# An encoder layer on one core: score products of the linear attention gathered in two visits a chunk, mLSTM scores placed behind the state products, output weights and gate transposes moved forward

## The chip, the cores and the metric

The kernel runs on one core of a Trainium2 chip. The metric is the device time of one execution in microseconds. The core's engines are TensorE (PE, matrix products), VectorE (DVE), ScalarE (ACT), GpSimd (POOL) and SyncE (SP, which here issues nearly all transfers). Each runs its own list of instructions in order and waits on semaphores for the others. Matrix products write to PSUM, which has eight banks of 512 numbers for each of the 128 partitions. TensorE's clock is granted by a throttle; the profile shows it as a share of full speed.

## The reference

One layer on 1024 tokens of width 1024. Token mixing: RMS norm, one input projection whose columns feed two groups of four heads, both scanned forward and backward with the directions summed, a norm for each head, a gate, one output projection, RMS norm, residual. Channel mixing: RMS norm, a gated MLP of width 2816 with a depthwise convolution of three taps, RMS norm, residual.

```
def hybrid_mixer(hn, w_in, ...):
    proj = jnp.matmul(hn, w_in).astype(jnp.float32)
    a_qk, a_v, a_o, a_gates, b_q, b_k, b_v, b_r, b_lr = jnp.split(proj, idx, axis=-1)
    ...
    y_a = jax.nn.sigmoid(a_o) * head_rms_norm(h_fw + h_bw, mlstm_norm).reshape(bsz, s, A_V)
    ...
    y_b = jax.nn.silu(b_r) * head_rms_norm(o_fw + o_bw, gla_norm).reshape(bsz, s, B_V)
    return jnp.matmul(jnp.concatenate([y_a, y_b], axis=-1), w_out)
```

The mLSTM group (a) has one decay for each token and head, so its scores are one product times a matrix of decays. The gated linear attention (GLA, group b) has a decay for each key dimension:

```
    diff = b[..., :, None, :] - b[..., None, :, :]
    decay = jnp.exp(jnp.where(causal, diff, -jnp.inf))
    s = jnp.einsum('bhtd,bhsd,bhtsd->bhts', q_, k_, decay)
```

## The kernel before, in words

The kernel works in chunks of 128 tokens (c = 0 to 7), with forward and backward on the two halves of the partitions. Products of full precision are made of three: high times high, high times low, low times high part.

Two Python generators, `proj()` and `mix()`, give the work until the output projection. `_interleave` takes a step of whichever has the smaller sum of weights, so the weights (`R_AUX`, `R_COLS`, `R_GLA`, `R_STATES`, `R_ML`, `R_OUT`, each times `W_PROJ`) set how many steps of projections go between two steps of the mixers. The order in which the generators issue is a first order; a scheduler behind them fixes the final list of each engine.

`proj()` holds the input projections that are left after the first stage. They fill TensorE while the mixers' other engines work: 384 products of 512 columns (`facc`, `f_block`) for keys and queries, then 1344 of 256 columns (`tacc`, `t_block`) for values and gates. Here they are called fillers.

`mix()` goes through these stages:

- `gla_decay()` and `gate_rows()`: the decays of both groups. `gate_rows` adds biases, takes logarithms, scans and exponentials on rows of 36 partitions (`gi`, `gf`, `rm`), and then transposes them in TensorE, chunk by chunk (`ptc`), into columns `cols`.
- `gla()`: `levels(0)`; `states()` (key transposes `ptk`, state products `U`, running states `slots`); then for each chunk `levels(c+1)` and `finish(c)`. `levels` builds the 128 x 128 scores from eight levels L = 64, 32, 16, 8, 4, 2, 1, 0. `weigh(L)` forms differences `D` on GpSimd, exponentials `E` on ScalarE, and weighted queries `Q` and keys (`K` for 32, the zero-padded `kz[L]` for 16 to 1) on VectorE. `pair_up` multiplies them into a PSUM tile `sc`. `keep` copies the tile into `Pt` or `acc` on ScalarE (64, 32, 16) or with a predicated copy on VectorE (8 and below). `finish` makes the output `o` from `Pt`, the decayed queries and the state, and its head norm.
- `mlstm()`: `states()` (keys by DMA, transposes `ptm`, state products `Um`, running states `mslots`), then for each chunk `decays(c)` (loads of keys `kko`, broadcast decay rows `RB` and `RI`, queries `qq`; 1.4 MB by DMA), `front(c)` (scores `sr`, weighed into `RB`) and `back(c)` (products `nd` with values and states, then `hs`, its norm and its store to `dya`).
- `out_weights()`: eight rows of output weights, 0.5 MB each, are loaded into `oraw`, multiplied by the gains and split into `woh` (ScalarE) and `wol` (VectorE); then `prep(0)` loads the mixers' results and gates (`yv`, `gv`), multiplies them and transposes them (`pt`) for the output projection (`oacc`).

Behind the interleaved part stand the output projection and channel mixing, which the change leaves alone.

## Time and profile before

| what | value |
| --- | --- |
| three runs | 1189.73, 1193.89 (median), 1195.28 us |
| the profiled execution | 1189.67 us, its span 1187.9 us |
| mean granted TensorE clock | 0.989 |
| busy: PE, DVE, ACT, POOL | 1151.1, 878.7, 591.4, 166.5 us |
| projections and gates | about 48 to 146 us |
| GLA: level products of chunk 0 and states, then the chunks | 129 to 183, 183 to 297 us |
| mLSTM: states, then the chunks | 304 to 323, 327 to 409 us |
| rest of the projections and output weights | 409 to 440 us |
| output projection | 440 to 575 us |
| channel mixing | 575 to 1188 us |

A row of groups reads: line, engine, operation, output and inputs by the program's names, shapes, count, then busy time, mean nanoseconds of one, and the idle time before them with what ended it. A row of the timeline or of the chain begins with its start and its length. L182 is line 182 of the kernel before. Matmuls are pipelined: each is shown with its full length, and the step from one start to the next is what it costs TensorE. Busy time of PE therefore contains the short gaps between matmuls that do not follow at the full rate.

### The profile page before, as it was taken

How to read it: one execution, taken by the hardware profiler on the slowest of the kernel's cores; microseconds unless marked ns; L12 is line 12 of the kernel's file. 1: busy time of each engine (PE TensorE's matmuls, PEld its weight loads, DVE VectorE, ACT ScalarE, POOL GpSimd, SP SyncE). 2: the span in 40 equal slices, each digit the busy share in tenths (PEclk: the TensorE clock that was granted, in tenths of full speed). 3: DMA queues.
4: the chain of work that ended last, by engine and by line, in shares of the span. 5: the costliest groups of instructions: out<-in, count | busy, mean ns of one | idle time of the engine just before them, and what ended most of it. 6: DMA issues, size and time to landing. Idle time of an engine off the chain costs nothing.

```text
span 1187.9 us, 21230 instructions
## 1 busy us (share of the span) xinstructions
PE 1151.1 (97%) x7896; PEld 979.7 (82%) x7896; DVE 878.7 (74%) x1604; ACT 591.4 (50%) x1271; POOL 166.5 (14%) x240
## 2 busy tenths in 40 slices
PE   8999999999999969999999999999999999999997
PEld 7989778888989968878788888888888878888885
DVE  5676669777433557667998888888888877987666
ACT  6572686878556534446543243433433245445451
POOL 1200425665054200101000000000000000000001
PEclk9999999999989989999999999999999999999999
DMA  7453675554777385542144342333224238754245
GB/s 201 149 134 102 169 223 155 152 171 127 189 197 209 117 278 186 178 141 80 36 142 142 109 132 64 113 123 108 89 81 133 98 123 299 252 178 133 81 137 190
DMA packets 134651, 175.77 MB, mean 148 GB/s; under 512 B 24964, under 2 KB 89860, under 8 KB 134548
## 3 DMA queue, kind: packets, MB, share of 16 engines
q1 hardware_dynamic: 134116, 172.58, 47.3%
q0 software_dynamic: 432, 1.84, 0.4%
q8 instruction: 62, 1.02, 0.3%
q14 instruction: 41, 0.34, 0.1%
HBM read 126.78 MB, written 47.53 MB: 147 GB/s over the span
## 4 chain that ended last, share of the span: by engine, by line
PE 73%; DVE 7%; ACT 6%; DMA 6%; issue 3%; POOL 3%; SPq 1%; DVEq 0%; POOLq 0%; ACTq 0%
PE pr L1063 35%; PE pr L1221 17%; PE facc L171 5%; PE oacc L1002 4%; PE tacc L182 4%; PE vacc L262 2%; DMA qq<-dmqq 1%; DMA yv<-dya 1%; DMA oraw<-in_w_out_dram 1%; DVE kz L637 1%; ACT sq L543 1%; DVE slots L537 1%; POOL RB L786 1%; POOL D L621 1%; POOL D L622 1%
## 5 line engine op out<-in xcount | busy, mean ns | idle before, releaser
L1063 PE MATMUL pr<-T,ah 128*128 128x512 f32 x704 | 217.2, 389 | 1.3 <-DVE G L1101 1.3
L1063 PE MATMUL pr<-B,ah 128*128 128x512 f32 x528 | 162.8, 390 | 0.0
L1063 PEld LDWEIGHTS pr<-T,ah 128*128 128x128 f32 x704 | 132.1, 188 | 29.4 <-DVE G L1101 1.8
L1063 PE MATMUL pr<-T,al 128*128 128x512 f32 x352 | 137.0, 389 | 0.0
L182 PE MATMUL tacc<-wh,xh 128*128 128x256 f32 x448 | 130.5, 291 | 0.0
L182 PE MATMUL tacc<-wl,xh 128*128 128x256 f32 x448 | 130.0, 290 | 0.0
L182 PE MATMUL tacc<-wh,xl 128*128 128x256 f32 x448 | 127.1, 284 | 0.0
L1221 PE MATMUL pr<-dwl,dah 128*128 128x512 f32 x308 | 120.0, 390 | 0.7 <-DVE dwl L113 0.7
L1221 PE MATMUL pr<-dwh,dal 128*128 128x512 f32 x308 | 120.1, 390 | 0.0
L1221 PE MATMUL pr<-dwh,dah 128*128 128x512 f32 x308 | 119.3, 390 | 0.0
L1063 PEld LDWEIGHTS pr<-B,ah 128*128 128x128 f32 x528 | 99.0, 188 | 20.4
L1063 PE MATMUL pr<-B,al 128*128 128x512 f32 x264 | 102.7, 389 | 0.0
L112 ACT CAST dah<-ar 128x512 fp32r<-128x512 f32 x77 | 47.6, 621 | 98.0 <-PE pr L1221 44.2
L182 PEld LDWEIGHTS tacc<-wh,xh 128*128 128x128 f32 x448 | 85.5, 191 | 2.7 <-issue 0.2
L182 PEld LDWEIGHTS tacc<-wl,xh 128*128 128x128 f32 x448 | 85.5, 191 | 1.4
L182 PEld LDWEIGHTS tacc<-wh,xl 128*128 128x128 f32 x448 | 85.7, 191 | 0.3
L112 ACT CAST ah<-fraw 128x512 fp32r<-128x512 f32 x64 | 39.6, 619 | 82.7 <-PE pr L1063 49.7
L113 DVE TENSOR_TENSOR dal<-ar,dah 128x512 fp32r<-128x512 f32 x77 | 53.0, 690 | 37.0 <-ACT dah L112 36.7
L1063 PEld LDWEIGHTS pr<-T,al 128*128 128x128 f32 x352 | 66.1, 188 | 13.6
L112 ACT CAST ah<-sa 128x512 fp32r<-128x512 f32 x44 | 27.4, 622 | 83.6 <-DVE sa L943 52.9
L1221 PEld LDWEIGHTS pr<-dwl,dah 128*128 128x128 f32 x308 | 57.8, 188 | 13.1 <-DVE dwl L113 1.1
L1221 PEld LDWEIGHTS pr<-dwh,dal 128*128 128x128 f32 x308 | 57.8, 188 | 12.9 <-DVE dal L113 0.9
(292 smaller groups left out, 2536.0 us busy)
## 6 DMA issues: line engine op xcount, KB each, us to landing
ar<-dA SPq DMA_DIRECT2D x77, 256.0 KB
wraw<-in_w_in_dram SPq DMA_DIRECT2D x48, 256.0 KB
fraw<-in_ffn_w_gate_dram SPq DMA_DIRECT2D x22, 512.0 KB
fraw<-in_ffn_w_up_dram SPq DMA_DIRECT2D x22, 512.0 KB
dA<-s SPq DMA_DIRECT2D x20, 512.0 KB
dA<-sx SPq DMA_DIRECT2D x10, 768.0 KB
Y<-in_ffn_w_down_dram SPq DMA_DIRECT2D x22, 256.0 KB
S<-dS SPq DMA_DIRECT2D x16, 258.0 KB
```

What stands on the lines that cost most here:

```text
L112: nc.scalar.copy(out=hi, in_=src)
L113: nc.vector.tensor_tensor(out=lo, in0=src, in1=hi.bitcast(F32), op=ALU.subtract)
L171: nc.tensor.matmul(acc, w[:, k, cs], v[:, k, hs], start=(k == 0 and n == 0), stop=(k == NK - 1 and n == 2))
L182: nc.tensor.matmul(acc[:, i, :], v[:, k, ts], w[:, k, :], start=(k == 0 and n == 0), stop=(k == NK - 1 and n == 2))
L262: nc.tensor.matmul(acc, v[:, k, ts], w[:, k, :], start=(k == 0 and n == 0), stop=(k == NK - 1 and n == 2))
L537: nc.vector.scalar_tensor_tensor(out=sl[rs, o, h, :], in0=sl[rs, c, h, :], scalar=sc(c, h)[rs], in1=sl[rs, o, h, :], op0=ALU.mult, op1=ALU ...
L543: nc.scalar.activation(sq, o[:, h, :], AF.Square, accum_out=ss[:, h:h + 1])
L621: nc.gpsimd.tensor_tensor(out=dv[:, :, :, 0, :], in0=ref, in1=xv[:, :, :, 0, :], op=ALU.subtract)
L622: nc.gpsimd.tensor_tensor(out=dv[:, :, :, 1, :], in0=xv[:, :, :, 1, :], in1=ref, op=ALU.subtract)
L1002: nc.tensor.matmul(accs[hf], v[:, j, :], w[:, k, hf * 512:(hf + 1) * 512], start=(k == 0 and n == 0), stop=(k == NK - 1 and n == 2))
L1063: nc.tensor.matmul(acc, A[i][:, k, :], B[b][j][:, k, :], start=(k == 0 and n == 0), stop=(k == 3 and n == 2))
L1221: nc.tensor.matmul(accs[i], o[v][:, ts], o[w], start=(p == 0 and n == 0), stop=(p == NP - 1 and n == 2))
```

## The change

Five things change, with the values computed staying the same.

1. **GLA scores in groups.** `products` takes up to five levels. The group's first is (64, 32, 16), which share one PSUM bank of 512 columns; the second is (8, 4, 2, 1, 0), which takes a bank and a quarter. `hold` puts the first product of a group behind a named instruction of the list, the weighing of the level after the group. For chunks 1 to 6 the second group, its copies and the last copies into `Pt` are put off (`owed`) until level 64 of the next chunk has been weighed. `Q` has eight buffers in place of three. The differences of each level are held behind the last filler issued so far (`pace`).
2. **mLSTM scores behind state products.** `front(c+1)` is issued directly behind the last `nd` product of chunk c, its weighing one step later. `decays(0)` and `decays(1)` are issued within the states, keys are loaded two chunks ahead, the next keys are transposed behind the state products, and `v` is loaded in `front`. `mslots` moves into the pool `ml`.
3. **Output weights.** Three of the eight rows get a pool of their own and are loaded at chunks 4, 5 and 6 of the mLSTM; each further row is loaded as soon as one has been split. `gpost` and the loads of `prep(0)` come earlier, the latter when the first half of the gates is done.
4. **Weights of the interleaving.** `R_AUX` 3.4 to 3.0, `R_GLA` 0.7 to 0.8, `R_ML` 1.9 to 1.7, `R_OUT` 2.0 to 1.3.
5. `yh` and `yl` of the output projection get a pool of their own.

```diff
-R_AUX, R_COLS, R_GLA, R_STATES, R_ML, R_OUT = 3.4, 0.6, 0.7, 0.7, 1.9, 2.0
+R_AUX, R_COLS, R_GLA, R_STATES, R_ML, R_OUT = 3.0, 0.6, 0.8, 0.7, 1.7, 1.3
...
+        def hold(ins, after):
+            tc.add_manual_dep(ins.ins, after.ins.name, mybir.DependencyInfo(mybir.DependencyClass.NoSync, mybir.DependencyReason.DATA),
+                              reason="one visit")
...
-                def products(pair):
-                    scs = [(L, pair_up(L, *qk)) for L, qk in pair]
+                def products(group, last):
+                    scs, room, first = [], 0, None
+                    for L, (Q, K, _) in group:
+                        n = 256 if L == 64 else 128
+                        if room < n:
+                            bank, room = ps.tile([P, 512], F32, name="sc", tag="ps"), 512
+                        sc = bank[:, 512 - room:512 - room + n].rearrange("p (h t) -> p h t", h=H)
+                        room -= n
+                        m = pair_up(L, Q, K, sc)
+                        first = first or m
+                        scs.append((L, sc))
+                    hold(first, last)
                     for L, sc in scs:
                         keep(L, sc)
...
                 due = []
-                for n, L in enumerate((64, 32, 16, 8, 4, 2, 1, 0)):
+                for L in (64, 32, 16, 8, 4, 2, 1, 0):
                     due.append((L, weigh(L)))
-                    if n % 2 == 0 and n:
-                        products(due[:2])
-                        due = due[2:]
+                    if L == 64 and c - 1 in owed:
+                        owed.pop(c - 1)(due[0][1][2])
+                    if L == 8:
+                        products(due[:3], due[3][1][2])
+                        due = due[3:]
                     yield
...
+                if 0 < c < NC - 1:
+                    owed[c] = lambda last: rest(group, last)
+                else:
+                    rest(group, end)
...
+                        with tc.issue_after(ins.ins):
+                            nxt = keys(*loaded[n + 1])
...
                     yield
+                    if n in (4, 6):
+                        decays(n // 2 - 2)
                     yield
...
             yield from states()
-            decays(0)
-            decays(1)
             yield R_ML * W_PROJ
-            front(0)
+            front(0)()
             for c in range(NC):
                 if c + 2 < NC:
                     decays(c + 2)
-                if c + 1 < NC:
-                    front(c + 1)
+                if NC - 4 <= c < NC - 1:
+                    load_raw(c - NC + 4)
+                ins = back(c)
+                after = front(c + 1, ins) if c + 1 < NC else None
                 yield
-                back(c)
+                if after:
+                    after()
                 yield
...
+    def load_raw(k):
+        if "raw" not in ow:
+            ow["raw"] = right.enter_context(tc.tile_pool(name="orw", bufs=3, side="right", reuse_waits="tile"))
+        raws[k] = ow["raw"].tile([P, D], F32, name="oraw")
+        nc.sync.dma_start(raws[k], w_out[:, k, :])
...
         for k in range(NK):
-            raw = op.tile([P, D], F32, name="oraw", tag=("yv", "yv", "gv")[k % 3], bufs=(2, 2, 1)[k % 3])
-            nc.sync.dma_start(raw, w_out[:, k, :])
-            split_scaled(woh[:, k, :], wol[:, k, :], raw, hg[:, k, :])
+            split_scaled(woh[:, k, :], wol[:, k, :], raws.pop(k), hg[:, k, :])
+            if k + 3 < NK:
+                load_raw(k + 3)
             yield
+        nc.sync.dma_start(gpost, rows_of(a["norm_mix_post"][0]))
+        while "half" not in done:
+            yield
+        first = prep(0)
+        next(first)
         while "gate" not in done:
             yield
-        for _ in prep(0):
+        for _ in first:
             pass
-        nc.sync.dma_start(gpost, rows_of(a["norm_mix_post"][0]))
```

What the lists of the engines make of it stands at three places. The first is TensorE in the GLA loop, the levels below 16 of a chunk and what surrounds them (`sc` the scores, `tacc` a filler, `o` the chunk's output). Before, eight or more fillers stand between one level and the next:

```order
L182 MATMUL tacc<-wh,xh 128x256
L656 MATMUL sc<-Q,kz_1445 32x32 x16
L182 MATMUL tacc<-wl,xh 128x256
L182 MATMUL tacc<-wh,xl 128x256
...
L656 MATMUL sc<-Q,kz_1446 32x32 x16
L654 MATMUL sc<-qq,kk 32x32 x16
L182 MATMUL tacc<-wh,xh 128x256
L699 MATMUL o<-v,Pt 128x128
L700 MATMUL o<-slots,qd 128x128
```

After the change the five levels stand together:

```order
L184 MATMUL tacc<-wh,xh 128x256
L661 MATMUL sc<-Q,kz_1400 32x32 x16
L661 MATMUL sc<-Q,kz_1401 32x32 x16
L661 MATMUL sc<-Q,kz_1402 32x32 x16
L661 MATMUL sc<-Q,kz_1403 32x32 x16
L659 MATMUL sc<-qq,kk 32x32 x16
L184 MATMUL tacc<-wl,xh 128x256
```

Of the runs of attention products that fillers separate there were 110 up to the output projection, and there are 67.

The second place is ScalarE's list from the last rows of `gate_rows` to the first columns (`cols` is the copy of `ptc`, `stg<-tacc` the copy of a finished filler block of 48 products). Before:

```order
L361 ACTIVATE rm<-rm 36x1024
L359 ACTIVATE gf<-gf 36x1024
L357 ACTIVATE lt<-lt 36x1024
L436 COPY stg<-tacc 128x512 x2
L112 CAST wh<-wraw 128x512
L374 COPY cols<-ptc 128x108
```

And after the change:

```order
L363 ACTIVATE rm<-rm 36x1024
L361 ACTIVATE gf<-gf 36x1024
L359 ACTIVATE lt<-lt 36x1024
L438 COPY stg<-tacc 128x512
L376 COPY cols<-ptc 128x108
L438 COPY stg<-tacc 128x512
```

The first `ptc` stands 48 fillers earlier: behind 192 `facc` and 72 `tacc` products, before behind 192 and 120.

The third place is SP's list behind the last store of the mLSTM (`dya_84<-hs`). Before:

```order
L547 DMA dya_84<-hs 128x512
L862 DMA oraw<-in_w_out_dram 128x1024 x3
L869 DMA gpost<-in_norm_mix_post_dram 128x1024
L862 DMA oraw<-in_w_out_dram 128x1024 x2
L486 DMA dG_67<-stg 128x4x256
L862 DMA oraw<-in_w_out_dram 128x1024 x3
L921 DMA fcw<-in_ffn_conv_wt_dram 128x66
L878 DMA gv<-dG_67 128x1024
L875 DMA yv<-dya_77 128x512
```

And after the change:

```order
L550 DMA dya_84<-hs 128x512
L916 DMA gpost<-in_norm_mix_post_dram 128x1024
L930 DMA yv<-dya_77 128x512
L931 DMA yv<-dyb_69 128x512
L904 DMA oraw<-in_w_out_dram 128x1024 x2
L488 DMA dG_67<-stg 128x4x256
L904 DMA oraw<-in_w_out_dram 128x1024 x3
L933 DMA gv<-dG_67 128x1024
```

Three of the eight loads of weights now stand ahead of this place, and the loads of `yv` stand ahead of the other five. The fillers behind the last `nd` product are 168, and were 180.

110 lines of the change are left out of this document (65 added, 45 removed).

## The prediction

> **What bounds the kernel now.** The first view is the page's head: what each engine does over the whole span.
>
> ```profile
> span 1187.9 us, 21230 instructions
> PE 1151.1 (97%) x7896; PEld 979.7 (82%) x7896; DVE 878.7 (74%) x1604; ACT 591.4 (50%) x1271; POOL 166.5 (14%) x240
> ```
>
> TensorE is busy 97% of the span, so a gain must come out of PE's own time or its few holes. The second view cuts the span into stages: projections and gates, the GLA loop, the mLSTM chunks, the tail before the output projection, and channel mixing.
>
> ```profile
> 48.00:146.00 98.00, 97.47 (x703) 82.51 (x705) 65.77 (x96) 49.80 (x94) 21.99 (x52) 1.00 0.45 125
> 190.00:297.00 107.00, 101.28 (x2250) 92.55 (x2251) 85.71 (x192) 83.55 (x224) 65.83 (x101) 1.00 0.51 151
> 327.00:409.00 82.00, 77.20 (x646) 72.45 (x645) 33.31 (x127) 46.84 (x164) 36.63 (x23) 0.96 0.65 183
> 409.00:440.00 31.00, 22.32 (x185) 22.00 (x183) 15.85 (x29) 13.88 (x24) 1.01 (x1) 0.90 0.69 233
> 575.00:1188.00 613.00, 605.28 (x2664) 499.73 (x2664) 503.41 (x760) 248.35 (x401) 6.87 (x11) 1.00 0.41 134
> ```
>
> The columns are window, length, then busy time of PE, weight loads, DVE, ACT and POOL, granted clock, DMA share, GB/s. The change touches 48 to 440. Behind it PE is dense (605 of 613 us), so what is won before 440 is won at the end one for one. The third view names what PE waits for: us in total, times, longest.
>
> ```profile
> PE pt L888 <- DVE yv L882: 8.9, 2, 8.7
> PE sc L656 <- DVE kz L637: 3.8, 5, 1.2
> PE nd L807 <- DVE RB L798: 3.1, 2, 2.9
> PE sc L652 <- DVE K L632: 1.7, 1, 1.7
> PE sr L797 <- DMA qq<-dmqq: 1.0, 1, 1.0
> PE ptk L586 <- DVE Q L582: 0.8, 1, 0.8
> ```
>
> One hole is large, the 8.9 us ahead of the first output transposes. The rest of the change's room is inside PE's busy time, in short visits that interrupt the projection matmuls.
>
> **Term 1: fewer visits.** A visit is a run of attention matmuls between two projection matmuls. Counted in the order of the two kernels there are 110 before and 67 after, 43 fewer: 38 from the GLA scores, five from the mLSTM scores that now stand behind the state products. The timeline prices one.
>
> ```profile
> 198.23 0.46 PE L656 MATMUL sc<-Q,kz 128*32 128x32 f32 x32
> 198.62 0.39 PE L182 MATMUL tacc<-wl,xh 128*128 128x256 f32 x1
> 198.84 0.28 PE L182 MATMUL tacc<-wh,xl 128*128 128x256 f32 x1
> 198.96 0.28 PE L182 MATMUL tacc<-wh,xh 128*128 128x256 f32 x1
> ...
> 199.76 0.46 PE L656 MATMUL sc<-Q,kz 128*32 128x32 f32 x32
> 200.15 0.39 PE L182 MATMUL tacc<-wh,xh 128*128 128x256 f32 x1
> ```
>
> From 198.62 to 200.15, 1.53 us, run eight tacc matmuls and one visit. A tacc alone steps by 0.12 (198.84 to 198.96), eight take 0.96. The 32 score matmuls take 0.26 (0.46 less the 0.20 that a single one lasts). The 0.31 left is what going there and back costs. 43 x 0.31 = **-13.3**. Bounds: only the slow step of the first tacc behind a visit (0.22 for 0.12) and as much on the way in saved, 0.2 a visit, -9; half as much again for visits that wait a little for their operand, -19. I take the measured one. Sharing a bank costs PE nothing in this sum, since a group's matmuls stand together and its readers come behind all of them.
>
> **Term 2: fillers.** 1176 instead of 1164 tacc matmuls stand before the last mLSTM state product, which I call T (409.0 in the trace): 12 x 0.12 = **+1.4**; they are missing behind it, which term 5 counts.
>
> **Term 3: the gate transposes come too early.** With R_AUX at 3.0 the first ptc stands behind 192 facc and 72 tacc, not 192 and 120. Their operand is the end of a chain on DVE and ACT that the change leaves as it is.
>
> ```profile
> 94.11 14.39 PE tacc L182 x120
> 107.46 0.68 DVE L360 TENSOR_SCALAR gf<-gf 36x1024 f32<-36x1024 f32 x1
> 108.43 0.25 PE L373 MATMUL ptc<-ident,gi 36*128 36x36 f32 x1
> ```
>
> Today gf is ready at 108.14 and PE arrives at 108.4: no wait, nothing to spare. 48 tacc fewer are 5.8 us, so PE arrives at 102.7. The decay products ahead of it shift a little earlier and with them DVE's queue, by about 1 us as I read the order: gf at 107.2, a new hole of 4.5 us (bounds 0, if the chain follows PE, and 5.5). What a hole does to the clock stands in two places of the trace.
>
> ```profile
> 332.00:336.00 4.00, 1.87 (x10) 1.64 (x11) 1.23 (x1) 2.49 (x9) 3.45 (x2) 0.85 1.01 217
> 336.00:340.00 4.00, 4.00 (x20) 3.55 (x21) 1.23 (x1) 1.91 (x5) 1.68 (x1) 0.50 1.02 252
> 340.00:344.00 4.00, 4.00 (x35) 3.77 (x34) 2.17 (x14) 2.15 (x10) 1.90 (x2) 0.80 0.30 98
> 432.00:436.00 4.00, 0.00 (x0) 0.00 (x0) 3.13 (x4) 3.32 (x4) 0.00 (x0) 0.72 0.74 225
> 444.00:448.00 4.00, 4.00 (x13) 3.19 (x12) 1.23 (x4) 0.59 (x1) 0.00 (x0) 0.57 0.88 264
> ```
>
> The wait of nd for RB, 2.9 us and over at 334.1, was followed by 6.8 us at half clock (twice what 0.85, 0.50 and 0.80 lack of 1, by 4 us each), 3.4 lost. The 8.9 us hole was followed by half clock up to 447.4 (0.57 in the last row), some 4 lost after PE resumed at 439.5. So a hole of 4.5 us would cost 3.4 more in perhaps 7 of 10 cases, by where it falls: 2.4. Term 3 is **+6.9**, between 0 and 9.
>
> The Trainium skill (TensorE: Matmul & The Clock Gate, The HAM clock gate) gives a free-running window of 3413 ns and half rate only after a whole idle one. By it a 4.5 us hole loses the clock in one case of three, and the sum would be 1.3 lower; the trace's 3 us hole, shorter than a window, already lost it, so the sum goes by the trace.
>
> **Term 4: the other waits before T.** The rows of PE's waits give 3.8 + 3.1 + 1.7 + 1.0 + 0.8 = 10.4 us up to T, five smaller ones 2.3, the lost clock 3.4: 16.1. In their place I expect: RB's own wait gone, as decays(0) and (1) are now loaded while the states run, with 1.0 left; K and the states 3.3 as before (1.8 and 1.5); kz 3, with longer groups but later products; mLSTM loads 1.5. That is 8.8, **-7.3** (bounds 0 and -12).
>
> **Term 5: the tail.** Today after T come hs, its store, and eight 0.5 MB weight rows through few buffers, one behind the other.
>
> ```profile
> 412.35 3.38 DMA dya<-hs
> 415.78 3.49 DMA oraw<-in_w_out_dram
> 419.30 1.16 ACT woh L108
> 420.48 1.29 DVE wol L109
> ...
> 427.66 4.94 DMA oraw<-in_w_out_dram
> ...
> 435.12 3.79 DMA yv<-dya
> 439.49 1.23 PE pt L888 x4
> ```
>
> The first pt comes at T+30.5. In the changed kernel three rows are there already; woh can start behind hs at about T+3.5. On SP the loads of yv stand ahead of rows 3 and 4, and the first waits for the store of hs: T+6.8. Rows 3 and 4 land at about T+10.5, are split (1.16 and 1.30), rows 5 to 7 land by T+18, three more splits on DVE and two silu steps end near T+21.5, and eight products of 0.3 with gv bring pt to T+23.7: **-6.8**. The 168 fillers behind T take 20.2, so the hole is 3.5 us, not 8.9. Bounds: T+20.2 (loads hidden, -10.3) and T+28 (rows 5 to 7 late and slow as the 4.94 row, -2.5). A 3.5 us hole keeps the clock in 6 of 10 cases by the same reading, of 4 us: **-2.4**.
>
> **Sum:** -13.3 + 1.4 + 6.9 - 7.3 - 6.8 - 2.4 = -21.5 us. The profiled execution took 1189.67 (span 1187.9 and 1.8 around it), 4.2 below the median 1193.89. It would become 1168.2, and the median 1172.4: **1172**.
>
> **Rivals.**
>
> *The mLSTM chunks become a matter of DMA.* Today a steady chunk is 48 tacc and 4.0 us of products, 10.1 us; with 36 tacc it would be 8.4.
>
> ```profile
> 345.00:380.00 35.00, 34.09 (x300) 32.10 (x300) 13.56 (x52) 20.58 (x74) 15.65 (x11) 1.00 0.73 202
> 324.00:328.00 4.00, 4.00 (x34) 3.80 (x32) 3.42 (x13) 0.60 (x1) 2.14 (x1) 1.00 1.00 236
> 395.71 3.06 PE tacc L182 x24
> 398.77 1.78 PE nd L807 x16
> ```
>
> 202 GB/s over 10.1 us are 2.0 MB a chunk; in 8.4 us that is 243 GB/s, and a full DMA stretch moved 236. Each chunk is then 0.2 us late, and the three early weight rows (1.6 MB) take 6.6 us more: +8, and +3 if RB waits again: 1183. Against it: the loads run two chunks ahead.
>
> *The GLA loop becomes bound by its operands.* DVE works 85.71 us of the loop's 107, which hold a little over seven chunks of 14.7: 11.8 a chunk. PE's new period would be 14.7 less 38 x 0.31 / 8, 13.2. The second visit waits for five levels at once, and the score matmuls for the last of them:
>
> ```profile
> L637 DVE TENSOR_TENSOR kz<-E,kk 64x256 f32<-64x256 f32 x70 | 29.2, 416 | 0.5
> L629 DVE TENSOR_TENSOR Q<-E,qq 128x512 f32<-128x512 f32 x42 | 28.9, 688 | 5.5 <-ACT E L624 5.0
> ```
>
> If the chain of POOL, ACT and DVE costs DVE more than 1.4 us of idling in a chunk, it and not PE sets the period; the gain of the whole change is gone from 3.0 us of wait in each of seven chunks, about the length at which the clock also falls. With 4.2 us in each: 1172 + 29 = 1201, slower. For it: DVE at 80% already. Against it: the Q products waited only 5 us in the whole loop, and the second visit is put off into the next chunk.
>
> *Everything fits.* The gate chain follows PE earlier and the tail's loads hide: -6.9 and -3.5 more, 1162.
>
> *The early weights don't come early.* If rows 0 to 2 wait for space that is freed only in the tail, 9.2 us of term 5 are lost: 1181.
>
> **Chances.** As forecast 0.58 (its own range 1164 to 1180), DMA 0.17, operands 0.08, everything fits 0.12, weights late 0.05. The range that leaves out two in ten: 1161 to 1189. A change under 0.5%, about 6 us, can't be told from none. Faster by more: 0.55 + 0.11 + 0.12 + 0.03 = 0.81; the same 0.12; slower 0.07.
>
> **What would show it.** Term 1: T near 397, tacc runs with two score visits a chunk, PE's period in the GLA loop near 13.2. Term 3: a row in PE's waits, ptc for gf, of about 4.5 us at 103, with a clock of 0.5 behind it. Term 4: no RB wait near 330. Term 5: the wait of pt for yv at about 3.5. Wrong if PE's waits for kz add up to more than 10 us, if qq or RB waits return in the mLSTM chunks, or if pt still comes 30 us behind T.

## The result, and the profile after

The changed kernel took 1199.57 us (median of 7 runs, 1197.91 to 1200.90), the kernel before in the same session 1191.92 (1189.73 to 1196.00). The ratio is 1.0059, 95% interval 1.0037 to 1.0081: slower by 0.6%, where 1172 was forecast. The profiled execution has a span of 1196.4 us, 8.5 more than before. The page's head and the windows by stage, with the same columns as before:

```profile
span 1196.4 us, 21161 instructions
PE 1144.2 (96%) x7896; PEld 981.5 (82%) x7896; DVE 887.5 (74%) x1604; ACT 590.1 (49%) x1271; POOL 169.7 (14%) x240
```

```profile
190.00:297.00 107.00, 99.93 (x2306) 94.90 (x2305) 90.10 (x196) 81.93 (x215) 70.41 (x106) 1.00 0.50 145
327.00:409.00 82.00, 67.94 (x554) 64.56 (x552) 34.78 (x117) 41.80 (x145) 34.46 (x21) 0.94 0.71 201
409.00:440.00 31.00, 28.07 (x225) 27.51 (x226) 14.46 (x43) 13.87 (x44) 3.03 (x3) 0.89 0.33 124
```

TensorE is busy for 7 us less, in a span that is 8.5 us longer: work was saved, and waiting took its place. The second row shows where: from 327 to 409 TensorE was busy 77.20 us before and is now 67.94, at a lower clock. The stages have moved in these windows: the mLSTM chunks of the changed kernel run from 339.8 to 425.7, so its third window, 409 to 440, holds the end of the chunks and only then 14 us of the tail. What TensorE waits for, in total, times, longest:

```profile
PE nd L850 <- ACT sq L546: 9.9, 3, 6.4
PE pt L943 <- DVE yv L937: 4.9, 2, 4.6
PE ptc L375 <- DVE gf L362: 4.0, 1, 4.0
PE nd L850 <- ACT stg L482: 2.3, 1, 2.3
PE sc L661 <- DVE kz L642: 2.0, 4, 0.9
PE ptm L766 <- DMA kk<-dmk: 2.0, 1, 2.0
PE nd L850 <- DVE RB L840: 1.4, 1, 1.4
PE nd L850 <- issue: 1.4, 1, 1.4
```

The `pt` wait fell from 8.9 to 4.9 and the `ptc` wait of 4.0 is the one forecast. Four rows are of `nd`, 15.0 us together, against 3.8 before (the row of 3.1 and one of 0.7). The names in them (`sq`, `stg`) are of instructions that ended last before `nd` began, and `nd` reads neither; the timeline below shows what held it.

From the starts and ends in the trace, stage by stage, after minus before. A filler is taken out at its step, 0.227 us for a `facc` and 0.12 for a `tacc` product, so that the column on the right holds only products, waits and clock:

| stretch | before | after | fillers before, after | difference without fillers | forecast |
| --- | --- | --- | --- | --- | --- |
| to the first level products | 129.3 | 136.2 | 231 facc + 192 tacc in both | +6.9 | +6.9 |
| GLA levels, states and chunks, to the last `o` | 167.2 | 165.2 | 153 + 502, 153 + 529 | -5.2 | -12.6 |
| mLSTM states, to the first `sr` | 30.5 | 38.4 | 146, 191 | +2.5 | 0 |
| mLSTM chunks, to the last `nd` (T) | 81.8 | 85.9 | 324, 264 | +11.3 | -8 |
| 12 more fillers before T | | | 1164, 1176 | +1.4 | +1.4 |
| T to the first `pt` | 30.7 | 25.2 | 180, 168 | -5.5 | -6.8 |
| behind it | 748.4 | 745.5 | | -2.9 | -2.4 |

(The forecast by the prediction's terms. Second row: 38 of the 43 visits and the kz row; fourth: five visits, RB's own wait, the clock lost behind it, the loads.) The mLSTM chunks alone hold the whole loss and more: in them TensorE waits 15.0 us where it waited 4.8, and loses 6.8 us to a halved clock where it lost 3.4.

Each column is one execution, and its small differences are not all of the change. Four runs below (e1, e2, e3, e7) have the same list on TensorE up to the first `sr`. Their first three stretches took 134.5 to 135.7, 165.1 to 166.7 and 35.1 to 36.4 us. So the first row is +5.2 to +6.9, the second -5.3 to -3.7, and the third -0.8 to +2.5, which is no cost of the change. In the last row these runs took 747.0 to 749.1, so -2.9 is not clear of the spread.

The timeline from 395 to 416, cut to the rows of one turn of the circle (start, length, engine, line, operation, and in brackets the idle time before it and what ended it):

```profile
395.72 1.22 DVE L840 SCALAR_TENSOR_TENSOR RB<-sr,RB 128x1024 f32<-128x1024 f32 x1
395.83 0.33 SPq L550 DMA_DIRECT2D dya<-hs  x1
...
397.24 0.58 SPq L820 DMA_DIRECT2D RB<-drr  x1
...
404.44 2.36 POOL L823 TENSOR_TENSOR RB<-RB,cin 128x1024 f32<-128x1024 f32 x1 [6.14 <-DMA RB<-drr]
...
406.84 2.44 ACT L827 ACTIVATE RB<-RB,cols 128x128 f32<-128x128 f32 x8 [9.35 <-POOL RB L823]
409.19 1.11 ACT L865 ACTIVATE hs<-nd,rd 128x128 f32<-128x128 f32 x4
409.57 1.13 DVE L866 SCALAR_TENSOR_TENSOR hs<-nd,rd,hs 128x128 f32<-128x128 f32 x4 [8.29 <-ACT hs L865]
410.61 1.22 DVE L840 SCALAR_TENSOR_TENSOR RB<-sr,RB 128x1024 f32<-128x1024 f32 x1
410.72 0.33 SPq L550 DMA_DIRECT2D dya<-hs  x1
...
411.93 3.78 PE L850 MATMUL nd<-v,RB 128*128 128x129 f32 x16 [6.39 <-ACT sq L546]
```

It reads as a circle. SP issues the store of `hs` at 395.83, when `hs` is done, and only then the loads of `RB` for the chunk after next, which stand behind it on SP. They are there at 404.4, 7.2 us after the second was issued (the one issued at 371.45 took 4.6); GpSimd adds the mask; ScalarE makes the exponentials (406.84). `hs` of the chunk in hand, whose `nd` products were ready at 400, stands behind these exponentials on ScalarE and comes at 409.19. On VectorE the weighing of the next chunk's scores stands behind that `hs`; `nd` waits for it until 411.93. And SP's next store waits for the same `hs`: 410.72, one turn of 14.9 us. The earlier stores were issued at 351.82, 360.56, 371.07 and 382.38: turns of 8.7, 10.5, 11.3 and 13.5 us, each a little longer. SP's own waits in the chunks show the first link (what waited, for what; total, times, longest):

```profile
SPq L550 <- DVE hs L866: 35.9, 7, 9.2
```

SP stood for 35.9 us at the stores of `hs`, with the later loads behind them. It stood there before as well, for 28.2 us at six of them in 327 to 409; what changed is which loads stand behind which store.

Two things stand otherwise in the list of SP than before. Before, its RB loads (R) and stores of `hs` (S) stood as `S RRRR S RR S RR S RR SSSS` from the first store on; now they stand as `S RR S R S RR S R S RR SSS`. The last pair is behind five stores instead of four, and two pairs have a store between their halves. The exponentials of chunk c+2 stand ahead of `hs` of c on ScalarE in both kernels, in the kernel before from chunk 2 on.

### The profile page after: what moved, and what is told of

It is laid out like the page before. It is cut to its first block, busy times and chain, and to the rows that moved or that the text cites. A ratio compares the mean times of both kernels' runs of the same rounds, so it can differ in the third digit from the quotient of the medians.

```text
span 1196.4 us, 21161 instructions
## 1 busy us (share of the span) xinstructions
PE 1144.2 (96%) x7896; PEld 981.5 (82%) x7896; DVE 887.5 (74%) x1604; ACT 590.1 (49%) x1271; POOL 169.7 (14%) x240
## 4 chain that ended last, share of the span: by engine, by line
PE 54%; DVE 6%; DMA 2%; issue 1%; ACT 1%; POOL 1%; SPq 0%; DVEq 0%; POOLq 0%; ACTq 0%
PE pr L1120 33%; PE pr L1278 17%; PE oacc L1059 2%; DMA yv<-dya 1%; DMA oraw<-in_w_out_dram 1%; DVE xr L1080 1%; DVE T L113 1%; DVE yv L937 1%; DVE oacc L1024 1%; POOL or L1072 1%; DVE om L1029 0%; PE nd L850 0%; DVE B L113 0%; PE tacc L184 0%; DVE yl L113 0%
## 5 line engine op out<-in xcount | busy, mean ns | idle before, releaser
L184 PEld LDWEIGHTS tacc<-wl,xh 128*128 128x128 f32 x448 | 87.5, 195 | 2.2 <-issue 1.7
L112 ACT CAST ah<-fraw 128x512 fp32r<-128x512 f32 x64 | 39.6, 619 | 82.5 <-PE pr L1120 51.4
L1120 PEld LDWEIGHTS pr<-T,al 128*128 128x128 f32 x352 | 66.1, 188 | 13.7
L1278 PEld LDWEIGHTS pr<-dwh,dah 128*128 128x128 f32 x308 | 57.8, 188 | 12.4 <-ACT dah L112 0.3
```

The costliest lines, as they stand in the source:

```text
L112: nc.scalar.copy(out=hi, in_=src)
L184: pace["mm"] = nc.tensor.matmul(acc[:, i, :], v[:, k, ts], w[:, k, :], start=(k == 0 and n == 0), stop=(k == NK - 1 and n == 2))
L1120: nc.tensor.matmul(acc, A[i][:, k, :], B[b][j][:, k, :], start=(k == 0 and n == 0), stop=(k == 3 and n == 2))
L1278: nc.tensor.matmul(accs[i], o[v][:, ts], o[w], start=(p == 0 and n == 0), stop=(p == NP - 1 and n == 2))
```

## The experiments

Lengths of the mLSTM chunks are taken from the first `sr` to the last `nd` of the profiled execution. "Not filled" is that length without 0.12 us for each filler in it and 4.0 us of products for each of the eight chunks. What is left is mostly the two last columns: TensorE's waits, and the clock lost, which is half of the time at half clock.

| run | time, us | ratio to before, 95% | mLSTM chunks | fillers in it | not filled | waits | clock lost |
| --- | --- | --- | --- | --- | --- | --- | --- |
| before | 1191.92 | | 81.8 | 324 | 10.9 | 4.8 | 3.4 |
| after | 1199.57 | 1.0059 [1.0037, 1.0081] | 85.9 | 264 | 22.2 | 15.0 | 6.8 |
| e1_store | 1193.11 | 1.0013 [0.9995, 1.0031] | 79.1 | 264 | 15.4 | 11.5 | 3.4 |
| e2_hsfirst | 1187.56 | 0.9969 [0.9950, 0.9989] | 79.2 | 264 | 15.5 | 10.3 | 5.1 |
| e7_sthf | 1185.68 | 0.9941 [0.9919, 0.9962] | 72.2 | 264 | 8.5 | 6.0 | 1.7 |
| e8_sthflate | 1183.47 | 0.9923 [0.9895, 0.9952] | 68.4 | 264 | 4.7 | 4.0 | 0 |
| e3_noraw | 1198.94 | 1.0085 [1.0053, 1.0116] | 87.5 | 264 | 23.8 | 16.1 | 6.8 |
| e6_oldml | 1193.33 | 1.0012 [0.9995, 1.0028] | 84.8 | 276 | 19.7 | 10.0 | 6.8 |
| e10_storeback | 1196.79 | 1.0048 [1.0031, 1.0065] | 86.2 | 324 | 15.3 | 7.7 | 3.4 |
| e14_beforehs | 1191.51 | 0.9982 [0.9964, 0.9999] | 81.7 | 324 | 10.8 | 3.8 | 5.1 |
| e11_ml1 | 1191.81 | 1.0005 [0.9989, 1.0022] | 78.7 | 194 | 23.4 | 13.5 | 8.5 |
| e13_moreproducts | 1200.12 | 1.0055 [1.0033, 1.0076] | 87.8 | 192 | 16.8 | 12.1 | 5.1 |
| e15_lessml | 1185.62 | 0.9925 [0.9898, 0.9952] | 68.5 | 228 | 9.1 | 5.2 | 3.4 |

(For e13 its 16 us of added products are taken out too.) The time is the median of all runs, the ratio is to the kernel before in the same session, and the lengths are of one execution, which is not always a typical one: that of e1 lies 3.2 us below the run's median, those of e2, e6 and e13 4.1, 3.7 and 4.8 above.

### The circle: the store, and the exponentials

**e1_store** issues the store of `hs` of chunk c one chunk later, behind the RB loads of chunk c+3. From the loads of chunk 4 on, SP's order is then that of the kernel before.

```diff
+            if i == 0:
+                return lambda: nc.sync.dma_start(dst, o.rearrange("p h e -> p (h e)"))
             nc.sync.dma_start(dst, o.rearrange("p h e -> p (h e)"))
...
-                    nc.sync.dma_start(RB[:, i], drr[i][c:c + 1].broadcast_to([P, H, P]))
+                    pace["rb"] = nc.sync.dma_start(RB[:, i], drr[i][c:c + 1].broadcast_to([P, H, P]))
...
-                head_norm(lp, hs, dya[c], 0, c)
+                stores[c] = head_norm(lp, hs, dya[c], 0, c)
...
+                if c - 1 in stores:
+                    m = stores.pop(c - 1)()
+                    if c + 2 < NC:
+                        hold(m, pace["rb"])
```

> The changed kernel with one move on SP: the store of hs of chunk c is issued one chunk later and stands behind the broadcast loads (RB) of chunk c+3, no longer ahead of them. Ring theory (each mLSTM chunk waits for a circle: hs, its store on SP, the RB load queued behind it, GpSimd's RB, ScalarE's exponentials, the next hs): the circle is cut, the stretch from the first sr to the last nd falls from 86 us to 62 to 68, the clock drops in it go, the whole from 1199.6 to about 1180 (1175 to 1187). Transfer theory (the loads of the chunks and of the early weight rows together fill the DMA engines): nothing is moved less, so the stretch stays at 83 to 87 us and the time at 1198 to 1201. Gate theory (the early gate transposes alone explain the loss): no change either.

**e2_hsfirst** leaves the code of the store and puts the exponentials of chunk c+2 behind `hs` of chunk c on ScalarE.

```diff
-                for i in range(2):
-                    for h in range(H):
-                        nc.scalar.activation(RB[:, i, h, :], RB[:, i, h, :], AF.Exp, bias=cols[:, c, 0, 32 * i + h:32 * i + h + 1])
...
+                def exps(behind=None):
+                    for i in range(2):
+                        for h in range(H):
+                            m = nc.scalar.activation(RB[:, i, h, :], RB[:, i, h, :], AF.Exp, bias=cols[:, c, 0, 32 * i + h:32 * i + h + 1])
+                            if behind:
+                                hold(m, behind)
+                return exps
...
                 ins = back(c)
+                if exps:
+                    exps(pace["hs"])
```

> The changed kernel with one move on ScalarE: the exponentials of chunk c+2 stand behind the hs scalings of chunk c instead of ahead of them, so hs no longer waits for a load. Ring theory: the same circle is cut at another place, the stretch from the first sr to the last nd falls to 62 to 72 us and the time to about 1182 (1175 to 1190). Transfer theory: 83 to 87 us and 1198 to 1201, as before the move.

**e7_sthf** makes both moves: the two diffs above together.

> The changed kernel with both moves, the store of hs behind the next RB loads on SP and the exponentials behind hs on ScalarE. Each alone took the mLSTM stretch from 86 to 79 us. If one circle with two ties holds the chunks, either cut opens it and both give little more: 77 to 79, time 1186 to 1189. If there are two circles that each hold it at about 11 us a chunk, cutting both frees it: 66 to 72, time 1177 to 1183.

Measured: 85.9 us became 79.1, 79.2 and 72.2. Each move takes 6.8 or 6.7 us, both together 13.7. Alone, each gave less than forecast (62 to 68, and 62 to 72), and e7 came to the upper edge of its 66 to 72. The lists say how clean this is. From the first `sr` on, e2 and e7 differ in SP's list alone: those 7.0 us are the store's. The move on ScalarE comes with small moves on VectorE and SP. By the ratios of all runs e1 takes 0.5% less than the changed kernel, e2 0.9% and e7 1.2%. PE's waits for `nd` in e1 and in e7 show what remains:

```profile
PE nd L852 <- DVE RB L842: 3.5, 1, 3.5
PE nd L852 <- issue: 3.4, 2, 3.0
PE nd L852 <- DVE rs_v L548: 2.6, 1, 2.6
PE nd L852 <- ACT sq L546: 1.9, 1, 1.9
```

```profile
PE nd L857 <- DVE RB L847: 3.2, 1, 3.2
PE nd L857 <- DMA RB<-drr: 1.9, 1, 1.9
PE nd L857 <- issue: 0.8, 2, 0.5
```

With the store moved, `nd` still waits 11.4 us in five chunks. With both links cut it waits 5.9, of which 3.2 are in the first chunk, ahead of any store; one wait of 1.9 for a load is left in the others, and two short ones. So two links of the circle are real, and they add. They explain the loss of the changed kernel: with both cut it takes 0.6% less than the kernel before.

**e10_storeback** goes the other way: in the kernel before, the second RB load of a chunk stands behind the store.

```diff
-                    nc.sync.dma_start(RB[:, i], drr[i][c:c + 1].broadcast_to([P, H, P]))
+                    m = nc.sync.dma_start(RB[:, i], drr[i][c:c + 1].broadcast_to([P, H, P]))
+                    if i and c > 2:
+                        hold(m, pace[0])
```

> The kernel before with one tie added on SP: the second RB load of chunk c+3 stands behind the store of hs of chunk c, the place that it has in the changed kernel. Ring theory: each chunk's load now waits for hs, the mLSTM stretch grows from 82 us to 86 to 92 and the time by 3 to 9 us, to 1195 to 1200. If that tie is harmless by itself and the changed kernel's other moves are needed: 1190 to 1193.

Measured: 86.2 us for 81.8 before, and 1196.79 us, as the circle forecast. The order of one transfer a chunk on SP costs the old kernel 4.4 us in the stretch and 0.5% in all.

**e14_beforehs** gives the kernel before e2's move, with the same diff.

> The kernel before with one move alone: the exponentials of chunk c+2 on ScalarE stand behind hs of chunk c (in the kernel before, too, they stand ahead of it). If hs behind the exponentials is a link of the circle in the kernel before as well, its mLSTM stretch falls from 81.8 to 73-78 us and the time to 1184-1187 us, without any other part of the change; if in the kernel before TensorE's work sets the stretch (71.3 us of it, 10.5 lost), stretch and time stay within 2 us of 81.8 and 1191.9.

Measured: 81.7 us for 81.8, and 0.9982 of the time, an interval that just ends at 1. The windows of that stretch, of e14 and of the kernel before:

```profile
326.50:408.20 81.70, 77.88 (x643) 73.63 (x644) 33.93 (x125) 45.71 (x164) 36.79 (x23) 0.94 0.69 186
```

```profile
327.00:408.80 81.80, 77.00 (x645) 72.37 (x644) 33.12 (x125) 46.84 (x164) 36.63 (x23) 0.96 0.65 183
```

TensorE is busy 77 of 82 us in both. The exponentials stood ahead of `hs` in the old kernel as well: the link was there and cost nothing. My reading is that its 48 fillers a chunk kept TensorE busy longer than the circle took, one store further back, to come round, and that with 36 fillers and a later RB load it became what sets the period. No run puts the 48 fillers back into the changed kernel.

### Other suspects for the same stretch

**e3_noraw** takes the loads of the first three rows of output weights out of the mLSTM chunks.

```diff
-                if NC - 4 <= c < NC - 1:
-                    load_raw(c - NC + 4)
...
+        for k in range(3):
+            load_raw(k)
```

> The changed kernel without the early weight rows: all eight are loaded in the tail. Ring theory: the mLSTM stretch stays within 3 us of 86, the tail loses what the early rows won (first output transposes some 6 us later behind the last nd), time about 1204 (1200 to 1208). Transfer theory: the stretch loses the 7 us or more that 1.6 MB take, and the tail takes back some 6: 1196 to 1200.

Measured: 87.5 us against 85.9, and 1198.94 us, not the 1204 forecast. The three rows are issued at 401.8 (two) and 409.8, where the changed kernel issues them at 388.9, 399.7 and 401.0: their own pool lets them run ahead of T (425.0) even so. The one row that left chunk 5 won nothing, which speaks against the theory that these transfers make the chunks late; that the stretch would be as long with none of them was not seen. They may reach single loads: the last RB load took 4.9 us in e3 (from 398.2) and 7.2 in the changed kernel, with rows at 399.7 and 401.0 behind it, though that the rows make this difference is not shown. In e1 the DMA engines were full (share 1.03, 249 GB/s) for the 6.7 us that the last RB load took. The time from T to `pt` stays at 25.2 us, so the calls in the chunks bring nothing: the pool alone does.

**e6_oldml** is the change with the mLSTM stage (states, `front`, `back`) of the kernel before.

```diff
             yield from states()
+            decays(0)
+            decays(1)
             yield R_ML * W_PROJ
-            front(0)()
+            front(0)
...
-                ins = back(c)
-                after = front(c + 1, ins) if c + 1 < NC else None
+                if c + 1 < NC:
+                    front(c + 1)
                 yield
-                if after:
-                    after()
+                back(c)
                 yield
```

> The changed kernel with the mLSTM of before (states, loads two chunks ahead issued behind the states, scores ahead of the fillers), the early weight rows kept. If the loss lies in the mLSTM part (stretch from the first sr to the last nd, counted for the same number of fillers, 43 us before and 54 changed): that stretch goes back to 42 to 46, time 1187 to 1191. If it lies elsewhere (early gates, early weight rows, interleaving): 1197 to 1200.

Measured: 1193.33 us, 1.0012 [0.9995, 1.0028], so the old mLSTM brings the whole time back to that of the kernel before, within the interval, between the two forecasts. That agrees with a loss that lies in the new mLSTM. Its stretch does not look so: 84.8 us with 276 fillers, 19.7 not filled where the kernel before has 10.9, although the store stands behind both RB loads again. This execution took 1197.03 us, one of the three longest of ten, so the stretch may be some 4 us longer than usual. Its trace shows another hold on SP: the stores of filler blocks (`dG<-stg`), ahead of later loads, waited 14.1 us in the stretch, where they waited 4.3 in the kernel before. That this is the rest of the difference was not tested.

**e11_ml1** sets R_ML to 1.0, so that 70 fillers move from the mLSTM chunks to behind T.

```diff
-R_AUX, R_COLS, R_GLA, R_STATES, R_ML, R_OUT = 3.0, 0.6, 0.8, 0.7, 1.7, 1.3
+R_AUX, R_COLS, R_GLA, R_STATES, R_ML, R_OUT = 3.0, 0.6, 0.8, 0.7, 1.0, 1.3
```

> The changed kernel with R_ML at 1.0 in place of 1.7: about 60 fillers (7 us of PE work) fewer in the mLSTM chunks, as many more behind them. Chain theory: the stretch from the first sr to the last nd stays within 3 us of 86 us, with PE idle for longer in it. PE theory: it falls by 7 us, to 79. The whole time by the chain theory: the 238 fillers behind the last nd take 28.6 us where the tail's own chain needs 25, so 1201 to 1205.

Measured: 78.7 us, 7.2 less for 8.4 us of fillers less, and 1191.81 us, not 1201 to 1205. Waits and lost clock stayed together at 22 us. That is against the circle as I had it, which should have stayed at 86. But the run did not change fillers alone. In the list of ScalarE the exponentials (`RB<-RB`) stood ahead of all four `hs` in the changed kernel, chunk by chunk:

```
L827 ACTIVATE RB<-RB,cols 128x128 x8
L865 ACTIVATE hs<-nd,rd 128x128 x4
L827 ACTIVATE RB<-RB,cols 128x128 x8
L865 ACTIVATE hs<-nd,rd 128x128 x4
```

and in e11 half of `hs` stands ahead of them:

```
L865 ACTIVATE hs<-nd,rd 128x128 x2
L827 ACTIVATE RB<-RB,cols 128x128 x8
L865 ACTIVATE hs<-nd,rd 128x128 x2
```

With the weights of the interleaving, the scheduler's order of the other engines moved too. So e11 says nothing clean on fillers.

**e13_moreproducts** was to settle it: R_ML 1.2 (192 fillers) and nine more score products a chunk, on TensorE alone.

```diff
-                    for h in range(H):
+                    for h in [0] * 9 + list(range(H)):
                         nc.tensor.matmul(sr[:, h, :], kk[:, h, :], qq[0:64, h, :], start=True, stop=True)
```

> The change with R_ML 1.2 (192 fillers between the first sr and the last nd product, nearly the 194 of the run with R_ML 1.0) and, in every mLSTM chunk, nine more score products that write the first head's scores into the same PSUM tile ahead of the four real ones, which overwrite them: 72 x .11 us = 7.9 us more of TensorE's time in that stretch, and no more work on any other engine or queue. Theory one, TensorE's own work sets the stretch once the circle's wait is passed: 78.7 + 7.9 = 86.6 us. Theory two, the circle of loads, exponentials and hs sets it, and fillers lengthen it through what they put on SP, ScalarE and VectorE: 78.7 us, 77 to 81, with TensorE's waits shorter by about the 7.9 us that it now spends on products.

The group of `sr` in e13's stretch (line, engine, operation, shapes, count, busy time, mean ns):

```profile
L836 PE MATMUL sr<-qq,kko 64*128 64x128 f32 x208 | 24.6, 272 | 0.0
```

The expectation mis-sized its own edit: each product shows as two matmuls (208 for 104), so 72 more are 144 matmuls and take 16.0 us (a chunk's `sr` goes from 0.8 us to 2.8), not 7.9. The stretch is 87.8 us: against e11, 9.1 more for 15.8 more of work (16.0, less two fillers), which is neither "all of it" nor "nothing". The lists moved here as well, and e13's have the store behind both RB loads and the exponentials ahead of the whole `hs`, as e1's have. Beside e1 it has 7.4 us more work and is 8.7 us longer. Read so, TensorE's work counts in full; read against e11, by somewhat over half, and by the ratios of all runs (1.0055 and 1.0005) by 6 us of the 15.8. How much of TensorE's own time enters the circle stays open.

**e15_lessml** asks the same of the best version (e8, below) with R_ML 1.4, 36 fillers fewer.

```diff
-R_AUX, R_COLS, R_GLA, R_STATES, R_ML, R_OUT = 3.0, 0.25, 0.8, 0.7, 1.7, 1.3
+R_AUX, R_COLS, R_GLA, R_STATES, R_ML, R_OUT = 3.0, 0.25, 0.8, 0.7, 1.4, 1.3
```

> The change with the store of hs behind the later loads, the exponentials behind hs and the first gates late (the best run so far, 1183.5 us) and R_ML 1.4 in place of 1.7, so that some 30 fillers leave the mLSTM chunks and stand behind them, where some wait for the output weights is left to fill. If a filler in the mLSTM chunks costs more than its own .12 us through its loads and stores in the queues, the stretch falls from 68.4 to about 62-64 us and the time to 1179-1182 us; if it costs only its .12 us, moving it gains nothing and the time is 1183-1185 us.

Measured: 68.5 us against 68.4, and 1185.62 us is not to be told from 1183.47. The equal lengths do not mean that fillers are free there. From the second chunk's `nd` on, e15 takes 52.6 us with 192 fillers and e8 55.9 with 216: 24 fillers, 2.9 us of work, made 3.3 us. The first chunk took the gain back. There `nd` waits 3.4 us for `RB`, in e8 1.3, and the half clock behind it (339.5 to 346.4) costs some 3 us, in e8 none. So, as far as two single executions show, TensorE's work sets the later chunks of the best version, and the first chunk's wait for `RB` is what is left to win.

### The gates, and a better version

**e4_late** puts the first `ptc` 36 fillers later, with R_COLS 0.25 so that the columns follow more closely.

```diff
-R_AUX, R_COLS, R_GLA, R_STATES, R_ML, R_OUT = 3.0, 0.6, 0.8, 0.7, 1.7, 1.3
+R_AUX, R_COLS, R_GLA, R_STATES, R_ML, R_OUT = 3.0, 0.25, 0.8, 0.7, 1.7, 1.3
...
         yield
+        yield
         for c in range(NC):
```

> The changed kernel with the first gate transposes 36 filler products (4.3 us) later, and closer together, so that PE does not arrive ahead of the gates' chain. If the wait of 4.0 us and the half clock behind it are a loss of their own: PE's wait for gf goes, the first score products of chunk 0 come 6 to 7.5 us earlier for the same number of fillers, time about 1193 (1191 to 1197). If the mLSTM circle absorbs it, because what is won ahead is waited away there: 1198 to 1200.

Measured: the `ptc` wait is gone, and T comes at 417.2 instead of 425.7. But the time is 1196.29 us, 1.0041 [1.0023, 1.0059], because one wait behind T has grown (`pt`, 6.0 for 4.9) and one is new:

```profile
PE pt L944 <- issue: 6.0, 1, 6.0
PE pr L1121 <- ACT oacc L1067: 4.1, 1, 4.1
```

The second is at the start of channel mixing: with the order as it now is, the first `pr` takes the PSUM bank in which the last `oacc` still waits to be read, 4.1 us.

**e8_sthflate** is e7 with the late gates: its two diffs and e4's.

> The same with the gate transposes 36 fillers later as well. Later gates alone took 3.3 us off the whole, with PE's wait for gf gone but 4 us more at the start of channel mixing in its profile. If that came by chance of the profiled execution: 5 to 7 us below the run with both moves. If the gates' gain is taken back further on: within 3 us of it.

Measured: 1183.47 us, 0.9923 [0.9895, 0.9952], 0.8% below the kernel before, with T at 407.3. It is the lowest median here, 2.2 us under e7, so within the 3 us of the second forecast, and not to be told from e7, e12 and e15 by the intervals. It still has the 4.1 us of `pr`. **e12_best** tried to win them with R_COLS 0.3, whose order ends on another bank.

```diff
-R_AUX, R_COLS, R_GLA, R_STATES, R_ML, R_OUT = 3.0, 0.25, 0.8, 0.7, 1.7, 1.3
+R_AUX, R_COLS, R_GLA, R_STATES, R_ML, R_OUT = 3.0, 0.3, 0.8, 0.7, 1.7, 1.3
```

> The changed kernel with both moves in the mLSTM and the later gate transposes (these at R_COLS 0.3 in place of 0.25). In the run with 0.25 the last output accumulator lay in the PSUM bank that the first product of channel mixing takes, and PE waited 4.1 us for its reader; here it lies in the other bank. If that wait is what took back the gain of later gates: it is gone, time 1178 to 1181. If the gain was lost elsewhere: 1183 to 1185.

Measured: 1184.65 us, 0.9936 [0.9912, 0.9959]. The wait of `pr` is gone, and the time behind the first `pt` is 4.7 us shorter. The GLA levels, states and chunks became 4.0 us longer with 12 more fillers (1.4 us) in them, so that `sr` first comes at 342.1 and not 338.9, and the mLSTM chunks 1.1 us longer with 12 fewer. Together that is as much: no gain.

### The GLA scores alone

**e5_glaonly** gives the kernel before the grouping of the scores: `products`, `hold`, `owed` and the eight buffers of `Q`, with the old weights and the old mLSTM (only `mslots` stays in its new pool).

```diff
-                    if n % 2 == 0 and n:
-                        products(due[:2])
-                        due = due[2:]
+                    if L == 64 and c - 1 in owed:
+                        owed.pop(c - 1)(due[0][1][2])
+                    if L == 8:
+                        products(due[:3], due[3][1][2])
+                        due = due[3:]
```

> The kernel before with the GLA part of the change alone (score products in two groups, the second put off into the next chunk, eight Q buffers, mslots in the pool of the mLSTM as in the change), the old weights of the interleaving, the old mLSTM and the old tail. If fewer visits pay by themselves as the changed kernel's trace shows (5.7 us between the last U and the last o, for the same number of fillers): 1183 to 1187. At the price of the prediction, 0.31 us for each of 38 visits: 1179 to 1182. If the groups only pay where other parts of the change prepare them: 1190 to 1193.

Measured: 1191.49 us, 0.9998 [0.9980, 1.0015], as the third forecast has it. The GLA chunks take 116.1 us with 10 + 488 fillers, against 115.8 with 10 + 502: less TensorE work in the same time. Its waits, and one second visit of the changed kernel, without the fillers from 207.67 on:

```profile
PE o L723 <- ACT Pt L697: 3.7, 3, 2.4
PE sc L659 <- issue: 3.1, 2, 2.5
PE tacc L184 <- issue: 2.0, 1, 2.0
```

```profile
206.00 1.30 PE L661 MATMUL sc<-Q,kz 128*32 128x32 f32 x128
207.28 0.46 PE L659 MATMUL sc<-qq,kk 128*32 128x32 f32 x32
...
210.89 0.28 PE L184 MATMUL tacc<-wh,xh 128*128 128x256 f32 x1 [1.64 <-issue]
```

The visits are grouped as the change says, 160 matmuls in 1.7 us, 206.00 to 207.67. What was won on the way in and out comes back as waits: of `o` for `Pt`, which is complete only behind the second group, and of the groups themselves. In the GLA chunks TensorE waits 10.5 us, 5.9 before, and behind three of these waits the clock is at half for 3.4 us each, which loses 5.1 us; before it lost none there.

**e9_glafill** is e5 with R_GLA 0.78, which moves 93 more fillers into the GLA chunks (14 + 577).

```diff
-R_AUX, R_COLS, R_GLA, R_STATES, R_ML, R_OUT = 3.4, 0.6, 0.7, 0.7, 1.9, 2.0
+R_AUX, R_COLS, R_GLA, R_STATES, R_ML, R_OUT = 3.4, 0.6, 0.78, 0.7, 1.9, 2.0
```

> The kernel before with the GLA part of the change alone, as in the run with that part only, and R_GLA at 0.78 in place of 0.7: about 85 fillers (10 us of PE work) more between the last U and the last o, and as many fewer behind the mLSTM. Chain theory (the GLA loop takes some 116 us whatever PE does, because the level chain of GpSimd, ScalarE and VectorE needs it, so fewer visits only make room): the stretch from the last U to the last o stays at 116 to 120 us although PE does 10 us more there. PE theory (PE's work sets the loop): 124 to 128 us. The whole time says little: the fillers are missing in the tail, 1188 to 1196.

Measured: 121.5 us in the GLA chunks, 5.4 more for 11.6 us of fillers more. So about half of them fell into gaps that e5 had, and the rest lengthened the loop: it lies between the two theories. Without fillers 49.1 us are left, against 53.3 before and 47.5 in the changed kernel: the grouping saves 4 to 6 us of TensorE's time where there are fillers to use it. With waits and lost clock taken out as well, the chunks have 47.4 us left before, 40.4 in the changed kernel, 39.6 in e5 and 39.5 in e9. So 33 visits fewer (51 to 18 in the changed kernel) save 7 to 8 us, 0.21 to 0.25 each, and what is missing to that is waits and clock. The time rose to 1200.49 us, 1.0075 [1.0054, 1.0095], above the 1188 to 1196 forecast, since the fillers are missing in the tail, where `pt` now waits 18.7 (`pr` has its 4.1 too):

```profile
PE pt L915 <- DVE yv L909: 18.7, 2, 17.9
```

## Why the prediction was wrong

**Term 4, the waits before T, failed.** It took the new order of the mLSTM for relief (`RB` loaded early, the scores ready) and priced the chunks by TensorE's work: 36 fillers and 4.0 us make 8.4 us a chunk, as the DMA rival says. (Its steady chunk of 10.1 us less 12 fillers would be 8.7, and at that the rival's own 0.2 us a chunk is gone.) The runs show the chunks on a circle through four engines, which in the last turn took 14.9 us; the stretch came out 11.3 us worse, fillers aside, where the term and the five visits there had about 8 better. The prediction's own sign of being wrong, RB waits back in the mLSTM chunks, came true: the weighed `RB` is what `nd` waits for in the turns of the circle. I had looked at what each `nd` waits for, and not at where the store of `hs` and the exponentials stand in the lists of SP and ScalarE. "The loads run two chunks ahead", as I held against the DMA rival, was the false step: on SP they stood behind a store that waits for `hs`. e1, e2 and e7 show the two links and their price, e10 the store's in reverse. Cutting both wins 13.7 of the 19.3 us between forecast and result in this stretch. Of the rest, the first chunk's wait for `RB`, which the term had as gone but for 1.0, took 3.2 to 4.1 us in e1, e2, e3 and e7, though 1.4 in the changed kernel's trace. The DMA rival named the right place and, but for single loads (e1, e3), the wrong cause, bandwidth: e8 moves 214 GB/s through the stretch, the changed kernel 170 (last column, e8 first):

```profile
338.90:407.30 68.40, 64.24 (x585) 61.58 (x584) 35.52 (x132) 39.28 (x145) 28.81 (x19) 1.00 0.79 214
```

```profile
339.80:425.70 85.90, 70.86 (x585) 67.40 (x584) 36.30 (x134) 39.06 (x146) 29.12 (x19) 0.92 0.58 170
```

**Term 1, the visits, was mis-sized.** It gave 0.31 us for each of 43. The GLA stage kept 5.2 us of the 12.6 forecast with the kz row, 0.14 us for each of 38 visits; e9, in the chunks alone, 4.2 us for 33. Two things make the difference. The saving itself is 0.21 to 0.25 us a visit once waits and clock are set apart, near the term's lower bound of 0.2: five visits as priced, 5 x 0.57 = 2.85 us, became one of 1.86 us (from 205.91, a filler's step behind the last filler, to 207.67, and 0.10 of a slow first filler). And part of it came back as the waits that e5 shows, with a halved clock behind them. The rival of the bound operands named this mechanism, but it cost only part of the gain and did not decide.

**Term 3, the early gates, was right**: 4.0 us of wait (4.5 forecast), half clock from 106.9 to 113.7 behind it, which loses 3.4 (2.4 forecast; 1.7 in e1, e2 and e7), and 5.2 to 6.9 us in all up to the first level products (6.9). That one trace gives exactly 6.9 is chance. e4 shows that the wait can be had back by 36 fillers.

**Term 5, the tail, was nearly right**: 25.2 us from T to `pt` (23.7 forecast), and a wait of 4.9 (3.5). The clock behind it gained 1.9 us of the 2.4: half clock lasts to 455.0, 4.1 us into the products, where it lasted 7.9. As e3 shows, the rows need not be asked for in the chunks; their own pool lets them run ahead of T. No run held them back behind T, so that they are what shortened the tail is not tested.

**Term 2** was right, and so was no change in the mLSTM states: the 2.5 us of the one trace (a wait of 2.0 for `kk` among them) are not in e1, e2, e3 and e7. The conclusion on chances was too sure by far: four terms were gains bounded from the side of TensorE, and none asked what the other lists would do with a chunk that TensorE finishes sooner.

## What to carry to other kernels

Before a chunk is priced by the busiest engine's work, walk once round the loop that its buffers close: store, next load, each engine's queue in list order, product, store. A store that waits for its data holds back every load behind it on the same queue, and an instruction for the chunk after next that stands ahead of one for the chunk in hand puts a load's whole latency on the path. In the kernel before, the second link cost nothing (e14), and the first 4.4 us as soon as the loads stood one store later (e10); with less work for TensorE both decided. When a weight of the interleaving is changed, compare the lists of all engines, not the count of fillers alone.

## What the runs showed of the hardware

Where TensorE's clock falls can be read closely here. Windows of the changed kernel, each a wait of `nd` and the products behind it (the three numbers at the end are clock, DMA share and GB/s):

```profile
359.50:361.70 2.20, 0.16 (x2) 0.00 (x0) 2.17 (x5) 2.20 (x9) 0.00 (x0) 1.00 0.23 86
361.70:366.20 4.50, 4.43 (x32) 4.23 (x33) 0.58 (x5) 0.82 (x6) 3.33 (x2) 0.63 0.74 241
...
395.50:397.00 1.50, 0.14 (x2) 0.00 (x0) 1.44 (x3) 1.41 (x9) 0.00 (x0) 1.00 0.21 81
397.00:401.00 4.00, 3.96 (x41) 3.75 (x41) 1.95 (x11) 0.48 (x1) 1.02 (x1) 1.00 0.55 155
405.40:411.90 6.50, 0.14 (x2) 0.00 (x1) 2.26 (x5) 4.96 (x20) 2.63 (x2) 0.90 0.61 203
411.90:417.40 5.50, 5.47 (x32) 5.28 (x33) 0.60 (x5) 0.00 (x0) 1.01 (x1) 0.50 0.08 28
```

A wait of 2.1 us was followed by a mean clock of 0.63 over 4.5 us (1.7 lost), one of 6.4 by 0.50 over 5.5, one of 1.4 by none; e8, whose waits in the stretch are at most 1.6 us, kept the clock at 1.00. There is no sharp limit between them. A wait of 1.8 us in e5 (at 289.0) and one of 1.9 in e4 (at 404.0) were followed by 3.4 us at half clock, one of 2.3 in e12 (at 389.8) and one of 2.1 in e3 (at 361.5) by none. The wait of `ptc`, 3.7 to 4.4 us, stands in eight runs (after, e1, e2, e3, e6, e7, e11, e13), and half clock followed it in all eight, for 3.4 or 6.8 us. The Trainium skill (TensorE: Matmul & The Clock Gate, Part 1) ties half rate to a whole idle window of about 3.4 us; here waits shorter than that already cost it, as the prediction had read from the wait of 2.9 us, and 1.8 is less still. The prediction's one case in three by that rule, for a hole like that of `ptc`, was eight of eight. A second thing not expected is the 4.1 us that the first `pr` of channel mixing waits for a PSUM bank in e4, e8, e9 and e15, and not in the changed kernel, e7 or e12. My reading is that the order of fillers and groups long before decides which bank the last product tile takes.
